# Channel mixers of a two-layer encoder trunk: chains T2 to T4 as products of 512 columns, their second half added by a transfer

## The chip, the core and the metric

The kernel runs on one core of a Trainium2 chip. The core has five engines with instruction streams of their own: TensorE (PE) multiplies 128x128 weight tiles with up to 512 columns and writes to the accumulator memory PSUM; VectorE (DVE) and ScalarE (ACT) do elementwise work, from and to the on-chip memory SBUF and PSUM; GpSimd (POOL) and SyncE (SP) mostly issue transfers (DMAs). Engines wait for each other through semaphores, and each runs its own instructions in order.

The metric is the device time of one execution in microseconds, the median of several runs. Lower is better.

## What is computed

Two transformer-like layers over 512 tokens of width 1024, batch 1, all in float32: a mixer (mLSTM or banded attention, each with attention to a memory), then a gated MLP with a causal convolution of width 3 over time. The change is in that MLP, the "channel mixer", which runs once per layer:

```python
def conv_ffn(h, w_up, conv_w, conv_b, w_down):
    u, g = jnp.split(h @ w_up, 2, axis=-1)      # w_up: 1024 x (2 * 2816)
    g = causal_dwconv(g, conv_w, conv_b)
    return (jax.nn.silu(g) * u) @ w_down        # w_down: 2816 x 1024

# in each layer:
x = x + conv_ffn(rmsnorm(x, norm_ffn_g[l]), ffn_w_up[l], ffn_conv_w[l], ffn_conv_b[l], ffn_w_down[l])
```

## The kernel before

**Three products for one.** TensorE's fast float32 form (fp32r) keeps fewer bits than float32, so each operand is split in a high part, a cast by ScalarE (`split`, L122), and a low part, the rest, a subtraction by VectorE (L123). `mm3` then issues three products: high by high (L166), high weights by low activations (L167) and low weights by high activations (L168).

**Tiles and steps.** Activations lie with the channels on the 128 partitions and the 512 tokens along the row. The 2816 hidden channels of a mixer are 22 tiles j. Tiles 0 to 4 are computed plainly (`plain`). From 5 on, `later` runs one `step` per tile, which computes the up and the gate block of the tile together by Winograd's variant of Strassen's scheme: the weights as 2x2 blocks (up and gate by two halves of the 1024 input channels), the activations as 2x2 blocks (two halves of the channels by two halves of 256 tokens), seven chains of products in place of eight. The weight forms are A11, A12, S1, S2, S3, A22 and S4 (class `Forms`); the sums of the activations are T1 to T4 (`forms`, with `self.sums`). One chain (`products`) is four `mm3` of 256 columns: twelve products.

**Accumulators of a step.** `r1` gathers A11 B11, then S2 T2, S3 T3 and A22 T4 on top of each other, and ScalarE copies its state to SBUF after each of the four (L796, L802, L812, L819). `r2` takes A12 B21; `r3` takes S1 T1 and later S4 B22. From the copies come `up` (the tile's up block) and `pre` (its gate block before the convolution). All three lie in banks of 512 columns, of which the chains use 256.

**The tail.** Step j finishes tile j-1 (class `Tail`): `last_block` adds `r3` to the second half of `up`; `first_tap` is ScalarE's scale and bias of `pre` (L652); `second_tap` and `third_tap` are VectorE's shifted multiply-adds (L645), the latter followed by the SiLU on ScalarE (L909); `gated` multiplies by `up` (L912); `split` splits the result for the down projection.

**Down projection.** In the steps that `DOWN` names (6 and 8 to 20) two blocks of twelve products of 512 columns run between the chains (`down_products`), one behind S2 T2 and one behind S3 T3. ScalarE copies each from PSUM (`add`, L735) and POOL issues a transfer that adds it to a spill in DRAM (L736). Steps 5, 7 and 21 have no such blocks. The last six hidden tiles are projected after the steps.

**Order.** Within the steps the order of PE, ACT and DVE is that of the code (`manual_schedule`): a step names the next tile's weight forms (`nxt`: `sums`, `split_second`, `sum_third`, `split_up`, `split_sums`, `sum_fourth`, `split_down`, `split_gate`, with subtractions at L847) and the tail's parts in their places. Where such an instruction would wait, the scheduler can put work that follows the steps in front of it. SP issues the weight loads; POOL issues the spills and, in the first mixer, at the start of each step the copies that lay out the bias rows of the attention (`bias_rows`, L1242 and L1244, of which the second waits for the first to land). Buffers come from pools: `t` has 8 tiles of 128x512, `bias` 4 (in the second mixer two of them hold the final gain), PSUM's `mm` 3, `sc` 3 and `tr` 2.

Of the kernel before, what the change touches and what calls it, by code (L numbers as in the profile page):

```python
# [16 lines left out]
P = 128  # L17
D = 1024
S = 512
# [32 lines left out]
def trunk(  # L52
# [572 lines left out]
    class ChannelMixer:  # L625
# [64 lines left out]
        def forms(self):  # L690
# [10 lines left out]
            for k in range(KT // 2):  # L701
                b1, b2 = xT[k], xT[k + KT // 2]
                pairs = []
                ta, tb = sb("t", [P, S]), sb("t", [P, S])
                for o, x, y in (
                    (ta[:, :H], b1[:, H:], b1[:, :H]),
                    (ta[:, H:], b2[:, H:], ta[:, :H]),
                    (tb[:, :H], b2[:, H:], b1[:, H:]),
                    (tb[:, H:], b2[:, :H], ta[:, H:]),
                ):  # L710
                    V.tensor_tensor(out=o, in0=x, in1=y, op=ALU.subtract)
                for t in (ta, tb):
                    hi, lo = sb("u", [P, S], F32R), sb("u", [P, S], F32R)
                    split(hi, lo, t)
                    pairs.append((hi, lo))
                self.sums.append(pairs)
                yield
# [41 lines left out]
        def t(self, i):  # L759

            i, h = divmod(i - 1, 2)
            return [tuple(x[:, h * H : (h + 1) * H] for x in p[i]) for p in self.sums]
# [22 lines left out]
        def step(self, j, w, nxt, tail):  # L785
# [5 lines left out]
            then(tail, "last_block", "first_tap")  # L791
            w.split_fourth()
            r1, r2, new.r3 = ps("mm"), ps("mm"), ps("sc")
            new.up, new.u3, new.pre = sb("t", [P, S]), sb("t", [P, S]), sb("t", [P, S])
            self.products(r1, w.a11, self.b(0, 0), True)
            A.copy(new.up[:, :H], r1[:, :H])  # L796
            then(tail, "second_tap")
            self.products(r2, w.a12, self.b(1, 0), True)
            V.tensor_tensor(out=new.up[:, :H], in0=new.up[:, :H], in1=r2[:, :H], op=ALU.add)
            then(tail, "third_tap")  # L800
            self.products(r1, w.s2, self.t(2))
            A.copy(new.up[:, H:], r1[:, :H])  # L802
            then(nxt, "sums")
            then(tail, "gated")
            then(nxt, "split_second", "sum_third")
            w.down_products(0)
# [4 lines left out]
            self.products(r1, w.s3, self.t(3))  # L811
            A.copy(new.u3[:, :H], r1[:, :H])  # L812
            V.tensor_tensor(out=new.pre[:, H:], in0=new.u3[:, :H], in1=new.r3[:, :H], op=ALU.add)
            then(nxt, "split_sums")
# [3 lines left out]
            self.products(r1, w.a22, self.t(4))  # L818
            A.copy(new.pre[:, :H], r1[:, :H])  # L819
            then(nxt, "split_down", "split_gate")  # L820
# [687 lines left out]
```

## Time and profile before

| | |
|---|---|
| median of three runs | 1209.37 us (1208.14 to 1210.49) |
| profiled execution | 1208.28 us, its span 1206.5 us |
| busy in the span | PE 99%, weight loads 87%, DVE 78%, ACT 59%, POOL 12% |
| granted TensorE clock, mean | 0.999 |
| transfers | 161.79 MB, 134 GB/s over the span |

The span runs from the first to the last instruction of the profiled execution; 1.8 us of its time lie around it. Rows of the timeline give the start in us, the duration, the engine, the line, the operation, the tiles out<-in, shapes, and in brackets the idle time ahead with what ended it. A product's duration reaches over the starts of the next ones, since products are pipelined; the distance from one start to the next is what a product adds to the time. Line numbers are those of the kernel before; `L166`, `L167`, `L168`, `L122`, `L123` are lines of helpers and stand for many places.

### The profile page before, as it was taken

To read this page: it belongs to the slowest core of one execution; us is meant where nothing else is said; L and a number is where in the kernel's file an instruction comes from. 1 tells how busy PE (TensorE), PEld (TensorE's weight loads), DVE (VectorE), ACT (ScalarE), POOL (GpSimd) and SP (SyncE) were. 2 spreads that over 40 slices of the span, in tenths; PEclk is the share of its full clock that TensorE was granted. 3 is DMA by queue.
4 is the path that set the end of the run, shared out by engine and by line. 5 is a ranking of instruction groups with operands and counts; after the bars stand their busy time and mean duration, and the time that the engine had idled before them with its cause. 6 is when DMAs were issued, how large, how long until landed. Compare 5 with 4: busy or idle time off the path is not lost.

```text
span 1206.5 us, 18758 instructions
## 1 busy us (share of the span) xinstructions
PE 1191.2 (99%) x7031; PEld 1055.1 (87%) x7031; DVE 938.8 (78%) x1719; ACT 711.9 (59%) x1253; POOL 139.5 (12%) x229
## 2 busy tenths in 40 slices
PE   8999999999999999999999999999999999999997
PEld 8898888888889999999888888888889999999986
DVE  6877688887978777777698888997896777777755
ACT  4547577654655555555565667775565555555545
POOL 0211101011011111111021000101101010111100
PEclk9999999999999999999999999999999999999999
DMA  8646413347565766665564313244845456666551
GB/s 277 200 112 144 91 54 79 109 147 193 123 151 141 161 159 147 153 145 130 148 193 129 93 53 101 68 132 153 194 101 135 114 131 140 141 140 135 121 156 70
DMA packets 206284, 161.79 MB, mean 134 GB/s; under 512 B 8328, under 2 KB 185966, under 8 KB 206194
## 3 DMA queue, kind: packets, MB, share of 16 engines
q1 hardware_dynamic: 184338, 120.78, 34.2%
q0 software_dynamic: 21856, 39.82, 17.7%
q8 instruction: 55, 0.90, 0.3%
q14 instruction: 35, 0.29, 0.1%
HBM read 132.04 MB, written 32.46 MB: 136 GB/s over the span
## 4 chain that ended last, share of the span: by engine, by line
PE 94%; ACT 3%; DVE 2%; DMA 0%; issue 0%; SPq 0%; DVEq 0%; ACTq 0%
PE pmm L166 18%; PE pmm L168 18%; PE pmm L167 18%; PE ptr L166 6%; PE ptr L167 6%; PE ptr L168 6%; PE psc L168 5%; PE psc L167 5%; PE psc L166 5%; PE psc L505 2%; PE ptr L1335 1%; ACT wh L122 1%; PE ptr L1356 1%; PE ptr L1357 1%; DMA u<-in_mem_dram 0%; PE ptr L574 0%
## 5 line engine op out<-in xcount | busy, mean ns | idle before, releaser
L166 PE MATMUL pmm<-u,wh 128*128 128x512 f32 (+1 forms) x968 | 336.6, 348 | 0.1
L168 PE MATMUL pmm<-u,wl 128*128 128x512 f32 (+1 forms) x968 | 333.5, 345 | 0.0
L167 PE MATMUL pmm<-u,wh 128*128 128x512 f32 (+1 forms) x968 | 333.2, 344 | 0.1
L123 DVE TENSOR_TENSOR wl<-wr,wh 128x1024 fp32r<-128x1024 f32 (+4 forms) x168 | 194.5, 1159 | 94.0 <-ACT wh L122 93.4
L122 ACT CAST wh<-wr 128x1024 fp32r<-128x1024 f32 (+4 forms) x168 | 167.7, 1000 | 96.1 <-PE pmm L167 42.1
L168 PEld LDWEIGHTS pmm<-u,wl 128*128 128x128 f32 x968 | 183.6, 190 | 21.1
L167 PEld LDWEIGHTS pmm<-u,wh 128*128 128x128 f32 x968 | 183.9, 190 | 18.4 <-DVE u L123 0.8
L166 PEld LDWEIGHTS pmm<-u,wh 128*128 128x128 f32 x968 | 183.7, 190 | 18.0 <-ACT u L122 0.5
L166 PE MATMUL ptr<-u,wh 128*128 128x512 f32 x272 | 106.7, 392 | 0.0
L167 PE MATMUL ptr<-u,wh 128*128 128x512 f32 x272 | 106.5, 392 | 0.0
L168 PE MATMUL ptr<-u,wl 128*128 128x512 f32 x272 | 105.8, 389 | 0.0
L736 POOL DMA_DIRECT2D xspill<-t x64 | 55.9, 873 | 411.6 <-ACT t L735 411.6
L166 PE MATMUL pmm<-u,u 128*128 128x256 f32 x296 | 84.5, 285 | 2.5 <-ACT t L812 2.5
L168 PE MATMUL pmm<-u,u 128*128 128x256 f32 x296 | 83.9, 284 | 0.2 <-DVE u L123 0.2
L167 PE MATMUL pmm<-u,u 128*128 128x256 f32 x296 | 83.8, 283 | 0.0
L123 DVE TENSOR_TENSOR u<-pt,u 128x512 fp32r<-128x512 f32 x102 | 69.9, 688 | 9.7 <-ACT u L122 7.1
L166 PE MATMUL psc<-u,wh 128*128 128x256 f32 (+1 forms) x232 | 76.1, 328 | 0.0
L735 ACT COPY t<-ptr 128x512 f32<-128x512 f32 x64 | 37.5, 585 | 65.4 <-PE ptr L168 65.4
L167 PE MATMUL psc<-u,wh 128*128 128x256 f32 (+1 forms) x232 | 75.9, 327 | 0.0
L123 DVE TENSOR_TENSOR u<-t,u 128x512 fp32r<-128x512 f32 x78 | 53.4, 689 | 22.0 <-ACT u L122 21.3
L122 ACT CAST u<-pt 128x512 fp32r<-128x512 f32 x102 | 63.0, 617 | 11.5 <-DVE pt L847 11.3
L909 ACT ACTIVATE t<-t 128x512 f32<-128x512 f32 x34 | 21.6, 634 | 80.3 <-DVE t L645 80.3
(282 smaller groups left out, 2562.5 us busy)
## 6 DMA issues: line engine op xcount, KB each, us to landing
wr<-in_ffn_w_up_dram SPq DMA_DIRECT2D x54, 512.0 KB, 4.9
wr<-in_ffn_w_down_dram SPq DMA_DIRECT2D x38, 512.0 KB, 3.8
pt<-in_ffn_w_up_dram SPq DMA_DIRECT2D x34, 512.0 KB, 6.7
xspill<-t POOLq DMA_DIRECT2D x64, 256.0 KB, 4.8
wr<-in_a_w_in_dram SPq DMA_DIRECT2D x20, 512.0 KB, 4.0
xspill<-u POOLq DMA_DIRECT2D x32, 256.0 KB, 2.9
u<-xspill SPq DMA_DIRECT2D x32, 256.0 KB, 5.2
wr<-in_w_kv_dram SPq DMA_DIRECT2D x12, 512.0 KB, 4.2
```

The lines of the kernel that those rows point to most:

```text
L122: high = A.copy(hi, src) if on_act else V.tensor_copy(hi, src)
L123: low = V.tensor_tensor(out=lo, in0=src, in1=f(hi), op=ALU.subtract)
L166: nc.tensor.matmul(o, lh, rh, start=first, stop=False, skip_group_check=more)
L167: nc.tensor.matmul(o, lh, rl, start=False, stop=False, skip_group_check=more)
L168: nc.tensor.matmul(o, ll, rh, start=False, stop=last, skip_group_check=more)
L505: nc.tensor.matmul(o, a, b, start=first and i == 0, stop=i == 1)
L735: A.copy(t, o)
L736: G.dma_start(xspill[j], t, accum_op=ALU.add)
L909: A.activation(self.acc, self.acc, AF.Silu)
L1335: nc.tensor.transpose(tp[:, b * P : (b + 1) * P], es[T, h][:, b * P : (b + 1) * P], ident)
L1356: nc.tensor.matmul(o2[:, s * P :], w, hi_at(pts[h], s, s, TT - s), start=s == 0, stop=False)
L1357: nc.tensor.matmul(o2[:, s * P :], w, lo_at(pts[h], s, s, TT - s), start=False, stop=s == TT - 1)
```

## The change

For tiles 5 to 20 of both mixers:

- The two parts of each of T1 to T4 now lie side by side in one tile of 512 columns (high in the first half, low in the second). For that, `forms` splits the sums in pieces of 256 columns.
- The chains of S2 T2, S3 T3 and A22 T4 are `wide_products`: per tile of input channels one product of the high weights with all 512 columns, and one of the low weights with the high half. The product of high weights and low activations gathers in the second half of `r1`'s bank.
- `fold` brings that second half in: ScalarE copies it to a `bias` tile (L774 of the changed kernel), and POOL issues a transfer that adds it to the destination in SBUF (L775): to the second half of `up` after T2, the second half of `pre` after T3, the first half of `pre` after T4.
- The parts of a step are reordered: the tail's `first_tap` and `second_tap` come behind the chain of T2, `third_tap` behind `split_second`; the next tile's `sums` come ahead of that chain, `sum_third` ahead of the first down block, `gated` behind it.

Tile 21 keeps the narrow chains, in the new order. PE has 6401 rows instead of 6785.

On ACT, step 7 of the first mixer (no down blocks), before. L796, L802 and L812 copy `r1` after A11 B11, S2 T2 and S3 T3; `t_3878` is the tail's tile, whose first tap stands ahead of this piece; `wh_3956` is the cast of `split_up`:

```order
L796 COPY t_3887<-pmm_3884 128x256
L909 ACTIVATE t_3878<-t_3878 128x512
L802 COPY t_3887<-pmm_3884 128x256
L122 CAST u_3935<-pt_3266 128x512
L122 CAST u_3952<-t_3878 128x512
L122 CAST wh_3956<-wr_3873 128x1024
L812 COPY t_3888<-pmm_3884 128x256
```

The same place in the changed kernel, where L821, L826 and L839 are those three copies, L774 the copies of `fold`, L652 the first tap and L938 the SiLU:

```order
L821 COPY t_3895<-pmm_3892 128x256
L826 COPY t_3895<-pmm_3892 128x256
L774 COPY bias_3935<-pmm_3892 128x256
L652 ACTIVATE t_3938<-t_3729,cols_772 128x512
L122 CAST u_3941<-pt_3266 128x512
L938 ACTIVATE t_3938<-t_3938 128x512
L122 CAST u_3961<-t_3938 128x512
L122 CAST wh_3965<-wr_3883 128x1024
L839 COPY t_3896<-pmm_3892 128x256
L774 COPY bias_3979<-pmm_3892 128x256
```

The first tap and the SiLU moved from ahead of the copy after T2 to behind it, and the copy after T3 has a second copy behind it.

On POOL, step 8 of the first mixer, before, from the second transfer of the step's bias rows on:

```order
L1244 DMA rep_4012<-maskf 64x64
L736 DMA xspill<-t_4108 128x512
L736 DMA xspill<-t_4151 128x512
L1242 DMA rep_4187<-in_b_rel_row_dram 128x640
L1244 DMA rep_4187<-maskf 64x64
```

The same place in the changed kernel, with the folds at L775:

```order
L1273 DMA rep_4019<-maskf 64x64
L775 DMA t_4035<-bias_4075 128x256
L736 DMA xspill<-t_4114 128x512
L775 DMA t_4037<-bias_4135 128x256
L736 DMA xspill<-t_4156 128x512
L775 DMA t_4037<-bias_4168 128x256
L1271 DMA rep_4191<-in_b_rel_row_dram 128x640
L1273 DMA rep_4191<-maskf 64x64
```

The three folds stand around the two spills, the first behind the bias rows' wait, the third ahead of the next step's bias rows.

Between the copies after T3 and T4 of step 21, PE had five products of the last down projection in the first mixer and six in the second; now it has nine and ten.

The diff:

```diff
@@ forms @@
-                for t in (ta, tb):
-                    hi, lo = sb("u", [P, S], F32R), sb("u", [P, S], F32R)
-                    split(hi, lo, t)
-                    pairs.append((hi, lo))
+                for t in (ta[:, :H], ta[:, H:], tb[:, :H], tb[:, H:]):
+                    both = sb("u", [P, S], F32R)
+                    split(both[:, :H], both[:, H:], t)
+                    pairs.append(both)
@@ t, wide_products, fold @@
         def t(self, i):
 
-            i, h = divmod(i - 1, 2)
-            return [tuple(x[:, h * H : (h + 1) * H] for x in p[i]) for p in self.sums]
+            return [(p[i - 1][:, :H], p[i - 1][:, H:]) for p in self.sums]
+
+        def wide_products(self, o, w, i):
+
+            n = KT // 2
+            for k in range(n):
+                both = self.sums[k][i - 1]
+                nc.tensor.matmul(o, w[0][:, k], both, start=False, stop=False, skip_group_check=True)
+                nc.tensor.matmul(o[:, :H], w[1][:, k], both[:, :H], start=False, stop=k == n - 1, skip_group_check=True)
+
+        def fold(self, to, o):
+
+            t = sb("bias", [P, S])[:, :H]
+            A.copy(t, o[:, H:])
+            G.dma_start(to, t, accum_op=ALU.add)
@@ step @@
             new = Tail(self, j)
-            then(tail, "last_block", "first_tap")
+            wide = j < FT - 1
+            then(tail, "last_block")
...
+            def chain(weights, i):
+                if wide:
+                    self.wide_products(r1, weights, i)
+                else:
+                    self.products(r1, weights, self.t(i))
+
+            def fold(to):
+                if wide:
+                    self.fold(to, r1)
+
             self.products(r1, w.a11, self.b(0, 0), True)
             A.copy(new.up[:, :H], r1[:, :H])
-            then(tail, "second_tap")
             self.products(r2, w.a12, self.b(1, 0), True)
             V.tensor_tensor(out=new.up[:, :H], in0=new.up[:, :H], in1=r2[:, :H], op=ALU.add)
+            then(nxt, "sums")
+            chain(w.s2, 2)
+            A.copy(new.up[:, H:], r1[:, :H])
+            fold(new.up[:, H:])
+            then(tail, "first_tap", "second_tap")
+            then(nxt, "split_second")
             then(tail, "third_tap")
-            self.products(r1, w.s2, self.t(2))
-            A.copy(new.up[:, H:], r1[:, :H])
-            then(nxt, "sums")
+            then(nxt, "sum_third")
+            w.down_products(0)
             then(tail, "gated")
-            then(nxt, "split_second", "sum_third")
-            w.down_products(0)
             self.products(new.r3, w.s1, self.t(1), True)
             w.add_down(0)
             then(tail, "split")
             then(nxt, "split_up")
-            self.products(r1, w.s3, self.t(3))
+            chain(w.s3, 3)
             A.copy(new.u3[:, :H], r1[:, :H])
             V.tensor_tensor(out=new.pre[:, H:], in0=new.u3[:, :H], in1=new.r3[:, :H], op=ALU.add)
+            fold(new.pre[:, H:])
             then(nxt, "split_sums")
             w.down_products(1)
             then(nxt, "sum_fourth")
             w.add_down(1)
-            self.products(r1, w.a22, self.t(4))
+            chain(w.a22, 4)
             A.copy(new.pre[:, :H], r1[:, :H])
+            fold(new.pre[:, :H])
             then(nxt, "split_down", "split_gate")
             self.products(new.r3, w.s4, self.b(1, 1))
```

## The prediction, made before the changed kernel was run

> **What bounds the kernel now.** I read the page first: busy times, granted clock and the chain that ended last.
>
> ```profile
> span 1206.5 us, 18758 instructions
> ...
> PE 1191.2 (99%) x7031; PEld 1055.1 (87%) x7031; DVE 938.8 (78%) x1719; ACT 711.9 (59%) x1253; POOL 139.5 (12%) x229
> ...
> PEclk9999999999999999999999999999999999999999
> ...
> PE 94%; ACT 3%; DVE 2%; DMA 0%; issue 0%; SPq 0%; DVEq 0%; ACTq 0%
> ```
>
> TensorE (PE) is busy for 99% of the span at full clock in all 40 slices, and 94% of the chain is its products. Busy time hides short waits, because one product's 0.28 us overlaps the next, so I then measured from one start to the next in the timeline of PE, over one step of the first channel mixer.
>
> ```profile
> 403.24 0.40 PE L166 MATMUL ptr<-u,wh 128*128 128x512 f32 x1
> ...
> 405.99 0.28 PE L166 MATMUL psc<-u,wh 128*128 128x256 f32 x1
> ...
> 407.42 0.28 PE L166 MATMUL pmm<-u,wh 128*128 128x256 f32 x1
> ...
> 418.80 0.40 PE L166 MATMUL ptr<-u,wh 128*128 128x512 f32 x1
> ```
>
> The rows at 403.24 and 405.99 enclose a block of the down projection: 12 products of 512 columns in 2.75 us, 0.229 us each. The rows at 405.99 and 407.42 enclose one chain: 12 products of 256 columns in 1.43 us, 0.120 us each. The row at 418.80 is the same place one step on, 15.56 us later. Seven chains and two down blocks are 7 x 1.44 + 2 x 2.75 = 15.58 us, so in such a step PE waits for nothing. The table by stage says the same of all the steps.
>
> ```profile
> 347.38:587.28 239.90, 238.65 (x1682) 224.40 (x1681) 183.65 (x268) 136.69 (x233) 38.77 (x53) 1.00 0.64 145
> 913.70:1153.60 239.90, 238.66 (x1682) 224.42 (x1681) 183.95 (x268) 136.90 (x234) 24.36 (x29) 1.00 0.57 130
> ```
>
> Each stretch runs from step 5 to the start of step 21 in one of the two mixers: 239.90 us each, PE busy 238.65. VectorE (DVE) is busy 183.65 and ScalarE (ACT) 136.69 of it. So PE's own time counts in full, ACT and DVE have room on average, and only a place where PE must wait for one chain of their work can cost anything.
>
> **What the merged products save.** Per chain of T2, T3 and T4, four products of 512 and four of 256 columns stand where twelve of 256 stood. The mean pitches give 4 x (0.229 + 0.120) = 1.40 against 1.44. A 512 right behind a 256 stands alone elsewhere in the trace.
>
> ```profile
> 221.32 0.28 PE L505 MATMUL psc<-u,u 128*128 128x256 f32 x1
> 221.43 0.40 PE L166 MATMUL pmm<-u,wh 128*128 128x512 f32 x1
> 221.67 0.52 PE L505 MATMUL psc<-u,u 128*128 128x256 f32 x3
> ```
>
> The 256 takes 0.11 and the 512 behind it 0.24 (the next row): 0.35 a pair, against 3 x 0.12 = 0.36. I take 0.35, so 0.04 us a chain and 0.12 us a step. The columns are the same, and only a fixed part of each product goes. The line through 0.120 at 256 and 0.229 at 512 puts that part at 0.011 us, which bounds the saving at 0.044 a chain; below, it is bounded by nothing saved. In the 28 steps with down blocks (14 in each mixer: 6 and 8 to 20) this is 28 x 0.12 = **-3.4 us** (ends -3.7 and 0).
>
> A rule speaks against even that. The Trainium skill, page "TensorE: Matmul & The Clock Gate", section "Wait — 56ns, not 53.3ns?", puts the fixed part of a product at about 2.5 ns at full clock. By it 384 fewer products would save an estimated 1.0 us, and the sum below would be about 2.5 us higher. The rows here speak for 0.011 us.
>
> **What the added copies and transfers cost in those steps.** Each step gains three ScalarE copies of 128x256, three transfers on GpSimd's (POOL) queue, and a later place for the tail's taps.
>
> ```profile
> 409.06 0.37 ACT L812 COPY t<-pmm 128x256 f32<-128x256 f32 x1 [0.82 <-PE pmm L168]
> 409.33 1.05 ACT L122 CAST wh<-pt 128x1024 fp32r<-128x1024 f32 x1
> ```
>
> The chain that began at 407.42 ended at 408.86, and the copy of its result starts 0.20 us behind it and gives way after 0.27. So 0.8 us of copies a step join ACT, which has over 6 us of room a step. Before a product overwrites a half, both copies must be done. In a step with down blocks the third chain is followed by 2.75 us of down products. Counted from the step's first product, T2's chain ends at 1.44 + 1.44 + 1.40 = 4.28 and the chain of T4 starts at 4.28 + 2.75 + 1.44 + 1.40 + 2.75 = 12.62 and the copies are done by 11.5 (worked out below for step 7, where they come at the same offset). They are hidden with 1.1 us to spare.
>
> The transfer behind T4's chain is the tight one, since the first tap of the next step waits for it.
>
> ```profile
> xspill<-t POOLq DMA_DIRECT2D x64, 256.0 KB, 4.8
> ...
> pt<-in_ffn_w_up_dram POOLq DMA_DIRECT2D x6, 512.0 KB, 7.2
> ...
> bias<-rep POOLq DMA_DIRECT2D x12, 256.0 KB, 3.2
> ```
>
> ```profile
> L736 POOL DMA_DIRECT2D xspill<-t x64: 850/859/944, 338.8 to 1150.9; - x64
> ...
> DMA to landing us min/median/max: 2.3/4.3/6.6
> ```
>
> None of these adds 128 KB from SBUF to SBUF. Adding 256 KB to DRAM lands after 4.8 us, adding 512 KB to SBUF after 7.2, a plain 256 KB into SBUF after 3.2. The line through the first two puts 128 KB at 3.6 us; the ends are 2.3 (fastest spill) and 7.2. I take 4.5, because the spill of add_down(1) is issued just ahead on the same queue. From T4's end to the issue it takes 0.20 + 0.27 + 0.37 = 0.84 us. The first tap could otherwise start 0.20 + 2 x 0.27 behind the chain of T2, which is 5.72 + 0.74 = 6.46 us after T4's end. So a landing up to 5.6 us after issue costs nothing, and with the 1.1 us above up to 6.7 us costs PE nothing. In the first mixer POOL also sits at a wait of its own.
>
> ```profile
> POOL rep L1244 <- DMA rep<-in_b_rel_row_dram: 62.6, 12, 6.3
> ```
>
> That is 12 waits, up to 6.3 us each, for the bias rows, now with the step's first fold queued behind them. The rows are issued behind the last fold, about 1 us into the step, so the first fold goes out near 8 us and lands near 12 of 15.4; its result is wanted at the next step's start. The cover is 3 us, so I cost it at nothing. The second fold waits for DVE's addition as well; behind it on POOL stands only the second spill, for which nothing waits in the step. Behind the first tap, should it wait, stand split_second's cast, the SiLU, a copy of the down block and so the whole tail.
>
> The finer splits of the sums (16 casts and 16 subtractions of 256 columns for 8 of each at 512, in each mixer) lie in the plain stage.
>
> ```profile
> 300.00:346.00 46.00, 46.00 (x206) 38.13 (x205) 40.52 (x67) 28.03 (x44) 4.78 (x5) 1.00 0.55 127
> ```
>
> PE is busy throughout it and DVE is idle for 5.5 of 46 us. On ACT a 256-column pass takes 0.27 to the next start where half of a 512 one takes 0.26 (rows above and below), and I estimate under 1 us in all on each engine. I cost that at nothing too; uncovered it would be 1 us.
>
> **Where the change loses.** Steps 5 and 7 of each mixer have no down blocks, so the chain of T4 follows that of T3 directly and waits for the copy of u3. Before, in step 7:
>
> ```profile
> 379.24 0.28 PE L168 MATMUL pmm<-u,wl 128*128 128x256 f32 x1
> 380.25 0.39 PE L166 MATMUL pmm<-u,u 128*128 128x256 f32 x1 [0.73 <-ACT t L812]
> ```
>
> The last product of T3's chain starts at 379.24 and ends its 0.12 at 379.36; T4's first starts at 380.25, 0.89 us of waiting for the copy at L812. Step 5 has the same place.
>
> ```profile
> 352.82 0.28 PE L168 MATMUL pmm<-u,wl 128*128 128x256 f32 x1
> 353.62 0.39 PE L166 MATMUL pmm<-u,u 128*128 128x256 f32 x1 [0.52 <-ACT t L812]
> ```
>
> Step 5 has no tail. There the fold's copy of 0.27 joins the wait of 0.68, and three chains save 0.12: **+0.15 us**, twice, +0.3.
>
> Step 7 has one, and the order of ACT has moved: the tail's first tap stands behind T2's copies instead of in front of the step, and the u3 copy still stands behind the SiLU, the tail's split and split_up. The durations come from step 7 of before.
>
> ```profile
> 376.76 0.63 ACT L909 ACTIVATE t<-t 128x512 f32<-128x512 f32 x1 [2.59 <-DVE t L645]
> ...
> 377.76 0.62 ACT L122 CAST u<-pt 128x512 fp32r<-128x512 f32 x1
> 378.36 0.62 ACT L122 CAST u<-t 128x512 fp32r<-128x512 f32 x1
> 378.88 1.04 ACT L122 CAST wh<-wr 128x1024 fp32r<-128x1024 f32 x1
> 379.83 0.36 ACT L812 COPY t<-pmm 128x256 f32<-128x256 f32 x1
> ...
> 383.71 0.81 ACT L652 ACTIVATE t<-t,cols 128x512 f32<-128x512 f32 x1
> 384.43 0.60 ACT L122 CAST u<-pt 128x512 fp32r<-128x512 f32 x1
> ```
>
> ```profile
> 375.65 0.74 DVE L645 SCALAR_TENSOR_TENSOR t<-t,cols,t 128x510 f32<-128x510 f32 x1
> 376.31 0.69 DVE L847 TENSOR_TENSOR pt<-pt 128x512 f32<-128x512 f32 x1
> ...
> 377.64 0.69 DVE L912 TENSOR_TENSOR t<-t,t 128x512 f32<-128x512 f32 x1
> ```
>
> On ACT: SiLU 0.63 (L909), cast to the next's start 0.52, the cast of 1024 columns 0.95 (378.88 to 379.83), first tap 0.81, L652. On DVE: a tap 0.74 or 0.66 to the next start (L645), a subtraction 0.60 to the next (376.31's kind), the gating product 0.69 (L912). From the step's first product: T2 ends at 4.28; its two copies run from 4.48 to 5.02; first tap to 5.83; second tap from 5.9 to 6.55; split_second's subtraction to 7.15; third tap to 7.9; SiLU to 8.55; gating to 9.3; tail's cast gives way at 9.85; split_up's at 10.8; u3's copy at 11.1; the fold's copy ends at 11.5. PE finished T3's chain at 4.28 + 1.44 + 1.40 = 7.12. It waits **4.4 us instead of 0.89**. Less the 0.12 saved, step 7 grows by 3.4 us. Adding pitches alone where I added full durations takes 0.6 off (2.8); hand-overs of 0.1 us instead of 0.05 put 0.3 on (3.7). PE has no idle later to give it back. Twice: **+6.8 us** (5.6 to 7.4).
>
> Step 21 keeps the narrow chains and its tail also comes later, but the scheduler fills that wait.
>
> ```profile
> 593.77 0.40 PE L167 MATMUL pmm<-u,wh 128*128 128x512 f32 x1
> 594.08 0.39 PE L166 MATMUL pmm<-u,u 128*128 128x256 f32 x1
> ```
>
> Five products of the last down projection stood there; the changed order has 9 in the first mixer and 10 in the second. They cover 9 x 0.229 = 2.06 us, up to 9.26 on the same clock, and the copy of u3 is done at about 9.4. I take +0.1 in all.
>
> **The sum.** -3.4 + 0.3 + 6.8 + 0.1 = **+3.8 us**. The profiled execution took 1208.28 us, a span of 1206.5 and 1.8 around it, so it would become 1212.1. That execution lies 1.1 below the median of the three runs, 1209.37; I predict the median, 1213.2. About 0.2% (2.4 us) is what a measurement of this kernel can tell from no change.
>
> **The rivals.**
> 1. The fixed part stays. If a 512 behind a 256 takes as long as two 256 (0.24, as in the row at 221.43, with 0.12 for the 256), nothing is saved in the 28 steps nor in steps 5 and 7: 3.8 + 32 x 0.12 = +7.6 us, 1217. Against it: the 256 ahead took 0.11 and the long runs 0.229. Chance 0.08. (The Trainium skill's 2.5 ns, page "TensorE: Matmul & The Clock Gate", would come out between this case and the forecast.)
> 2. The folds land late. If T4's transfer needs 7.2 us, as the 512 KB did, instead of under 6.7, the first tap, and with it the copies of u3, hold PE up 0.5 us in each of 28 steps: +14, 1227. For it: the spill landed after up to 6.6 us. Against it: half the bytes. Chance 0.13, most of it near the threshold (1214 to 1221).
> 3. On the other side: the weight load is what spaces the products of 256.
>
> ```profile
> L167 PEld LDWEIGHTS pmm<-u,wh 128*128 128x128 f32 x968 | 183.9, 190 | 18.4 <-DVE u L123 0.8
> ```
>
>    A load takes 0.19 us, longer than the pitch of 0.12, and a third of a chain's loads go. If a pair took 0.327, its columns at the slope of the line with no fixed part, a chain would save 0.132 and 96 chains 12.7 us: 7.6 - 12.7 = -5.1, 1204.3, faster. It decides from 0.08 us saved a chain (7.6 over 96). Against it: the lone pair at 0.35, and that 512-column products still carry the 0.011 although their loads have twice the time. Chance 0.05.
> 4. The wait in step 7 is mostly filled or shorter, so that gain and loss cancel: its added part would have to fall from 3.4 to below 2.7 us for less than 0.2%. The order of PE shows nothing between T3 and T4 there; only the times can do it. Together with the noise of a median, chance 0.14.
>
> **How the numbers follow.** My forecast has 0.60, with a range of its own of 1211 to 1215. With rivals 1 and the near part of 2 above it and part of 4 below, 1210.2 to 1218 leaves out about 0.2. Slower by over 0.2%: most of the forecast (0.55), rivals 1 and 2, 0.76. Within: 0.18, of rival 4 and the forecast's low end. Faster: rival 3 and a little of 4, 0.06.
>
> **What would show it.** Right: steps with down blocks of 15.43 to 15.45 us instead of 15.56; step 7 at about 14.6 us instead of 11.2, with T4's first product waiting over 4 us for ScalarE; a transfer of the fold landing in under 5.6 us with the first tap waiting for PE alone; 96 ScalarE copies without a wait of PE behind them elsewhere. Wrong: a down step above 15.6 us (folds late, or nothing saved at 15.56), or T4 in step 7 waiting under 3 us.

## The result, and the profile after

The changed kernel takes **1242.43 us** (median of five runs, 1236.80 to 1245.46) against 1209.37 before: a ratio of 1.0271 (95% interval 1.0255 to 1.0287), 33 us slower. The prediction had the sign, but said 1213.2 us, 1210.2 to 1218.0. The profiled execution of the changed kernel is the fastest of the five, 1236.80 us; its span of 1235.0 us is 28.5 us longer than the one before, and that is the part that the trace explains.

The page of the changed kernel, its lines on the span, the engines' busy time, the granted clock, the chain that ended last (by engine, then by line) and the folds' transfers (KB each, median us from issue to landing):

```profile
span 1235.0 us, 18341 instructions
...
PE 1199.1 (97%) x6647; PEld 1037.1 (84%) x6647; DVE 941.3 (76%) x1735; ACT 740.3 (60%) x1365; POOL 225.6 (18%) x325
...
PEclk9999999999999999999999999999999899999989
...
PE 60%; DMA 14%; issue 9%; DVE 8%; ACT 7%; POOL 2%; SPq 0%; ACTq 0%; POOLq 0%; DVEq 0%
...
t<-bias POOLq DMA_DIRECT2D x96, 128.0 KB, 3.5
```

PE's products were 94% of the chain and are 60%; transfers, which had 0%, hold 14%. PE is still 97% busy, and its busy time is even 8 us larger (1191.2 before): the clock fell in some slices, and a product at half clock counts as busy too. So the busy share hides most of this loss.

The table by stage, from step 5 to the start of step 21 in each mixer (length, then busy time of PE, PEld, DVE, ACT, POOL, granted clock, DMA share, GB/s):

```profile
346.82:596.39 249.57, 241.89 (x1490) 214.40 (x1489) 183.78 (x267) 149.08 (x280) 81.64 (x101) 0.99 0.77 162
926.16:1175.89 249.73, 241.15 (x1490) 214.45 (x1489) 183.79 (x266) 149.36 (x281) 66.34 (x77) 0.99 0.71 147
```

Each of these stages was 239.90 us. Going from one step's first ScalarE copy to the next one's, the extra 28.5 us lie as follows. "Down steps" are those with down blocks; "step 21" reaches to the next mixer's step 5, or to the end.

| us more than before | mixer 1 | mixer 2 |
|---|---|---|
| up to step 5 | -0.56 | (in step 21 of mixer 1) |
| step 5 (10.94 before) | +0.08 | +0.10 |
| step 7 (11.20 before) | +5.37 | +6.45 |
| down steps, 14 in each | +4.22 | +3.28 |
| step 21 and what follows | +3.35 | +6.20 |

**Down steps: the third fold lands late.** The place where one step passes to the next, mixer 2, in the timeline of POOL, then the landing time of the third of these transfers and of the spill ahead of it, then the next instruction on ScalarE that needs the third, then all such waits of ScalarE (total, times, longest):

```profile
1124.24 0.86 POOL L775 DMA_DIRECT2D t<-bias  x1 [2.83 <-ACT t L735]
1124.78 1.21 POOL L736 DMA_DIRECT2D xspill<-t  x1
1125.36 1.52 POOL L775 DMA_DIRECT2D t<-bias  x1
```

```profile
DMA to landing us min/median/max: 6.4/6.4/6.4
```

```profile
DMA to landing us min/median/max: 6.3/6.3/6.3
```

```profile
1131.79 0.82 ACT L652 ACTIVATE t<-t,cols 128x512 f32<-128x512 f32 x1 [1.01 <-DMA t<-bias]
```

```profile
ACT t L652 <- DMA t<-bias: 37.0, 26, 3.7
```

Second fold, spill and third fold are issued within 1.1 us. The third lands 6.4 us after its issue, at 1131.76, and the first tap (L652) starts at 1131.79. ScalarE waits there in 26 of 32 steps, 37 us in all. The spill, issued 0.58 us ahead of the fold, landed 0.7 us ahead of it. In 23 of the 28 steps with a spill it is the same: the third fold lands 0.6 to 1.0 us behind the spill issued ahead of it (1.2 to 2.1 in the others), whether that spill went out 0.6 or 1.5 us earlier. The spills themselves take 5.2 to 7.3 us. The length of a step follows from the landing of the third fold issued at the end of the step ahead of it. In mixer 2, with the landing first: 5.3 gives a step of 15.54 us, 6.4 gives 15.52 to 15.65 (five steps), 6.7 gives 15.87, 7.1 gives 16.30, 7.2 gives 16.35, 7.5 gives 16.64. (One lands after 6.1, but was issued 0.5 us later in its step: 15.77.) From about 6.4 us on, what the landing gains the step gains.

**Steps 7 and 21: PE waits, and then runs at half clock.** PE in the second mixer: the last product of T3's chain and the first of T4's in step 7, the last filling product and the first of T4's in step 21.

```profile
958.12 0.28 PE L769 MATMUL pmm<-u,wl 128*128 128x256 f32 x1
964.28 0.80 PE L768 MATMUL pmm<-u,u 128*128 128x512 f32 x1 [5.88 <-ACT bias L774]
...
1183.52 0.39 PE L166 MATMUL pmm<-wh,u 128*128 128x512 f32 x1
1187.71 0.58 PE L166 MATMUL pmm<-u,u 128*128 128x256 f32 x1 [3.81 <-ACT t L839]
```

The table by stage behind these two waits, and behind the shorter one of step 21 in the first mixer (2.98 us idle):

```profile
964.28:968.75 4.47, 4.46 (x20) 4.09 (x21) 2.76 (x4) 2.40 (x5) 1.42 (x2) 0.62 0.30 47
1187.71:1192.99 5.28, 5.28 (x24) 5.28 (x25) 2.10 (x4) 1.19 (x2) 0.00 (x0) 0.50 0.64 178
607.16:608.69 1.53, 1.53 (x12) 1.53 (x13) 0.94 (x3) 0.00 (x0) 0.00 (x0) 1.00 0.10 29
```

After 5.88 us of idleness the granted clock is 0.62 on average for 4.5 us (0.50 for the first 3.4), after 3.81 it is 0.50 for 5.3 us, after 2.98 it is 1.00. So the 6.2 us from step 21 of mixer 2 on are, to a few tenths, a wait of 3.8 and half of 5.3.

### The profile page after: what moved, and what is told of

It reads as the page before. It is cut to its first block, busy times and chain, and to the rows that moved or that the text cites. A ratio compares the mean times of both kernels' runs of the same rounds, so it can differ in the third digit from the quotient of the medians.

```text
span 1235.0 us, 18341 instructions
## 1 busy us (share of the span) xinstructions
PE 1199.1 (97%) x6647; PEld 1037.1 (84%) x6647; DVE 941.3 (76%) x1735; ACT 740.3 (60%) x1365; POOL 225.6 (18%) x325
## 4 chain that ended last, share of the span: by engine, by line
PE 60%; DMA 14%; issue 9%; DVE 8%; ACT 7%; POOL 2%; SPq 0%; ACTq 0%; POOLq 0%; DVEq 0%
DMA t<-bias 13%; PE pmm L166 11%; PE pmm L167 11%; PE pmm L168 11%; PE pmm L768 3%; PE psc L168 3%; PE psc L167 3%; PE psc L166 3%; PE ptr L166 3%; PE ptr L168 3%; PE ptr L167 3%; DVE t L645 3%; ACT wh L122 2%; PE psc L505 2%; ACT t L652 2%
## 5 line engine op out<-in xcount | busy, mean ns | idle before, releaser
L166 PE MATMUL pmm<-u,wh 128*128 128x512 f32 (+1 forms) x840 | 300.5, 358 | 0.1
L168 PE MATMUL pmm<-u,wl 128*128 128x512 f32 (+1 forms) x840 | 297.4, 354 | 0.0
L167 PE MATMUL pmm<-u,wh 128*128 128x512 f32 (+1 forms) x840 | 297.1, 354 | 0.1
L167 PEld LDWEIGHTS pmm<-u,wh 128*128 128x128 f32 x840 | 159.2, 190 | 18.2 <-DVE u L123 0.8
L166 PEld LDWEIGHTS pmm<-u,wh 128*128 128x128 f32 x840 | 159.1, 189 | 18.1 <-ACT u L122 0.5
L775 POOL DMA_DIRECT2D t<-bias x96 | 97.0, 1011 | 190.5 <-ACT bias L774 90.6
L645 DVE SCALAR_TENSOR_TENSOR t<-t,cols,t 128x511 f32<-128x511 f32 x80 | 59.7, 747 | 75.8 <-ACT t L652 75.7
L768 PE MATMUL pmm<-u,u 128*128 128x512 f32 x256 | 97.3, 413 | 16.3 <-ACT bias L774 15.8
L768 PEld LDWEIGHTS pmm<-u,u 128*128 128x128 f32 x256 | 49.1, 192 | 34.1 <-ACT bias L774 24.7
L769 PE MATMUL pmm<-u,u 128*128 128x256 f32 x256 | 72.9, 285 | 0.0
L123 DVE TENSOR_TENSOR u<-t,u 128x512 fp32r<-128x512 f32 (+1 forms) x94 | 53.9, 597 | 24.8 <-ACT u L122 24.4
L122 ACT CAST u<-t 128x512 fp32r<-128x512 f32 (+1 forms) x94 | 49.1, 544 | 23.6 <-DVE t L941 11.0
```

The costliest lines, as they stand in the source:

```text
L122: high = A.copy(hi, src) if on_act else V.tensor_copy(hi, src)
L123: low = V.tensor_tensor(out=lo, in0=src, in1=f(hi), op=ALU.subtract)
L166: nc.tensor.matmul(o, lh, rh, start=first, stop=False, skip_group_check=more)
L167: nc.tensor.matmul(o, lh, rl, start=False, stop=False, skip_group_check=more)
L168: nc.tensor.matmul(o, ll, rh, start=False, stop=last, skip_group_check=more)
L645: V.scalar_tensor_tensor(acc[:, n:], src[:, : S - n], self.fw[:, c * FT + j : c * FT + j + 1], acc[:, n:], op0=ALU.mult, op1=ALU.add,)
```

## The experiments

Three theories had to be told apart: the transfers of the folds, the new order of the step, and the merged products themselves. Times are medians; the ratio is against runs of the kernel before on the same chip (1208.75 us in the first four, 1208.21 in the next four, 1209.35 in the last two).

| run | us | ratio (95%) |
|---|---|---|
| 1 order only | 1219.29 | 1.0084 (1.0069 to 1.0099) |
| 2 no transfer | 1221.40 | 1.0100 (1.0085 to 1.0116) |
| 3 folds by VectorE | 1232.70 | 1.0195 (1.0178 to 1.0212) |
| 4 old steps 5 to 7 and 21 | 1215.52 | 1.0054 (1.0036 to 1.0072) |
| 5 no transfer, filler | 1216.06 | 1.0064 (1.0050 to 1.0078) |
| 6 spill later, first try | 1256.00 | 1.0388 (1.0366 to 1.0409) |
| 7 third fold by VectorE | 1220.72 | 1.0102 (1.0088 to 1.0116) |
| 8 old steps, third fold by VectorE | 1207.76 | 0.9998 (0.9989 to 1.0008) |
| 9 spill behind the third fold | 1222.72 | 1.0117 (1.0101 to 1.0132) |
| 10 old steps, spill behind the third fold | 1207.71 | 0.9994 (0.9985 to 1.0003) |

### 1. Order only

All chains narrow, no folds, the changed kernel's order.

```diff
-            wide = j < FT - 1
+            wide = False
```

> The changed kernel in its new order, but with narrow chains for every tile, so without merged products, copies and transfers of the fold. Theory O (the new order costs in the steps without down blocks): step 7 keeps a wait of about 4 us ahead of T4's chain and step 21 one of 1 to 3 us, down steps are 15.56 us, in all +6 to +12 us against before (ratio 1.005 to 1.010). Theory F (late folds cost everything): within 2.4 us of before. If the longer down blocks of the changed kernel (2.78 us for 2.74) come from the merged products ahead of them, they are back at 2.74.

Measured: 1219.29 us, 10.5 more than before. Steps 7 take 16.41 and 15.48 us instead of 11.20; T4 waits 3.66 us for ScalarE's copy of u3 (L839) in both, with half clock behind it (the chain of S4 takes 2.56 and 2.09 instead of 1.44). The same wait costs 0.9 us more in one mixer than in the other, as the granted clock stood at 0.50 for 6.8 us in the first and for 3.4 us in the second. Every down step is at 15.55 to 15.57, and the down blocks are back at 2.75 us. Step 21 is filled (0.18 us idle), so the 1 to 3 us expected there did not come. So the order alone costs its price in step 7, and nowhere else.

### 2. No transfer

Merged chains and the copies, but the second half is not added, so `up` and `pre` miss the low part of the sums.

```diff
             A.copy(t, o[:, H:])
-            G.dma_start(to, t, accum_op=ALU.add)
```

> The changed kernel without the 96 transfers of the fold; the copies from PSUM stay, and the second half's part of the sums is left out of the output. Theory F (the third fold lands late, 6.4 us after issue, and holds the first tap): the first tap waits for no transfer, down steps are 15.54 us in place of 15.86 in the mean, about 9 us below the changed kernel from these steps alone and some 2 more from step 7 and 21, so +20 to +23 us against before. Theory O alone: the down steps and the time stay at +33.

Measured: 1221.40 us, a ratio of 1.0100 where the changed kernel has 1.0271: the transfers cost some 21 us. It is 12.7 us above before where 20 to 23 were expected. In the profiled executions step 21 accounts for much of that: its 9.5 us more than before become 1.0, where some 2 us were expected of steps 7 and 21 together. The first copies of steps 8 and 20 of mixer 2, in run 1 and then in run 2:

```profile
960.62 0.37 ACT L821 COPY t<-pmm 128x256 f32<-128x256 f32 x1 [1.13 <-PE pmm L168]
...
1147.34 0.37 ACT L821 COPY t<-pmm 128x256 f32<-128x256 f32 x1 [0.52 <-PE pmm L168]
```

```profile
964.68 0.37 ACT L820 COPY t<-pmm 128x256 f32<-128x256 f32 x1 [1.67 <-PE pmm L168]
...
1151.16 0.37 ACT L820 COPY t<-pmm 128x256 f32<-128x256 f32 x1 [0.25 <-PE pmm L168]
```

Twelve steps take 186.72 us with narrow chains and 186.48 with merged ones: 15.56 and 15.54 a step. **The merged products save 0.02 us a step**, 12 products fewer at 1.7 ns each, instead of the 0.12 forecast. The merged chains themselves are shorter (T2 and T3 1.41 instead of 1.44, T4 1.40 instead of 1.43), but the down block behind T2 and the one behind T3 each take 2.78 instead of 2.75.

Step 7 of the first mixer, T3's last and T4's first product, and the table by stage from there on:

```profile
380.25 0.28 PE L769 MATMUL pmm<-u,wl 128*128 128x256 f32 x1
384.76 0.79 PE L768 MATMUL pmm<-u,u 128*128 128x512 f32 x1 [4.23 <-ACT bias L774]
```

```profile
384.76:390.05 5.29, 5.29 (x21) 4.90 (x22) 3.45 (x5) 3.22 (x6) 0.00 (x0) 0.50 0.23 75
390.05:392.92 2.87, 2.87 (x26) 2.87 (x25) 2.06 (x4) 0.68 (x2) 0.00 (x0) 1.00 0.48 148
```

The wait beyond the pitch of 0.12 is 4.38 us: the 4.4 of the prediction, to the hundredth or two. But then PE runs 5.3 us at half clock (6.1 in the other mixer), and the step takes 16.82 us (17.16 in the other mixer), not 14.6.

### 3. All folds by VectorE

```diff
-            t = sb("bias", [P, S])[:, :H]
-            A.copy(t, o[:, H:])
-            G.dma_start(to, t, accum_op=ALU.add)
+            V.tensor_tensor(out=to, in0=to, in1=o[:, H:], op=ALU.add)
```

> The changed kernel with the fold done by one VectorE addition from PSUM in place of the copy and the transfer. Theory F: as without transfers, +18 to +23 us against before, if VectorE's 3 x 0.33 us a step more stay hidden. Rival: VectorE is the next to hold PE, and the down steps stay above 15.7 us.

Measured: 1232.70 us. All down steps take 15.83 us. PE in one of them, the end of the second down block and the first product of T4, and then VectorE's addition of T3's second half:

```profile
1014.14 0.39 PE L168 MATMUL ptr<-u,wl 128*128 128x512 f32 x1
1014.61 0.47 PE L768 MATMUL pmm<-u,u 128*128 128x512 f32 x1
1014.91 0.28 PE L769 MATMUL pmm<-u,u 128*128 128x256 f32 x1
```

```profile
1012.38 1.22 DVE L123 TENSOR_TENSOR wl<-wr,wh 128x1024 fp32r<-128x1024 f32 x1 [0.26 <-ACT wh L122]
...
1014.04 0.42 DVE L773 TENSOR_TENSOR t<-t,pmm 128x256 f32<-128x256 f32 x1
```

T4's first product starts 0.47 us behind the last of the block instead of 0.23, and the next one 0.30 behind it instead of 0.24. T3's addition on VectorE (1014.04, 0.42 us) stands behind a subtraction of 1024 columns and ends at 1014.46; T4 may not write the half before that. So the rival holds, that VectorE is the next to hold PE: giving all folds to VectorE trades a late landing for a late release of the accumulator: 28 times 0.29 us, and a T4 wait of 5.77 us in step 7.

### 4. The old order in steps 5 to 7 and 21

Those steps narrow and in the order of before; tiles 8 to 19 merged with transfers; step 20 narrow in the new order.

```diff
-            wide = j < FT - 1
-            then(tail, "last_block")
+            wide = 8 <= j < FT - 2
+            old = j < 8 or j == FT - 1
+            then(tail, "last_block", *(["first_tap"] if old else []))
...
+            if old:
+                then(tail, "third_tap")
+                chain(w.s2, 2)
+                A.copy(new.up[:, H:], r1[:, :H])
+                then(nxt, "sums")
+                then(tail, "gated")
+                then(nxt, "split_second", "sum_third")
+                w.down_products(0)
+            else:
...
```

> Merged products and folds only for tiles 8 to 19; steps 5 to 7 and 21 in the order of before, the others in the new order. Theory O: step 7 is back at 11.2 us, step 21 waits for nothing beyond before, and PE is at full clock throughout; left over is the lateness of the folds, 12 steps in each mixer of about +0.3 us: +6 to +9 us against before. Theory F: the time stays within 6 us of the changed kernel.

Measured: 1215.52 us (1211.82 to 1219.35, a wide spread for this program). Steps 5 and 7 are back at 10.93 and 11.20. In the profiled execution the second mixer's steps 8 to 19 are all at 15.54, the first one's between 15.52 and 17.14. In the second mixer the third folds land in 5.2 to 5.8 us up to step 18, and no step is held up; the second spill goes out 1.2 to 1.9 us ahead of them. In the first mixer they land in 6.3 to 7.3 us from step 9 on, with the spill 0.6 us ahead. So the same steps run in two ways. My reading of the trace: a late tap makes the tail late, the second fold, which waits for VectorE's addition, goes out later, the spill behind it moves up to the third fold, and that fold lands late again; once begun, it keeps itself up. How it begins is not shown: in step 9 of the first mixer, the first with a late fold, the tap was on time and the second fold went out 0.8 us later in the step than in the second mixer all the same. The reading would also explain why the changed kernel's own runs spread over 8.7 us, where those without transfers spread over 2.7.

### 5. Products in place of idleness

Run 2, and in step 7 eighteen products ahead of T4's chain, whose results are not used.

```diff
             w.add_down(1)
+            if j == 7:
+                for _ in range(18):
+                    nc.tensor.matmul(r2, w.s1[0][:, 0], self.ready[0][0], start=True, stop=True)
             chain(w.a22, 4)
```

> The kernel without the fold's transfers (the second halves are not added), in which step 7 took 16.82 and 17.16 us and T4's chain waited 4.38 us in both mixers; now 18 products of 512 columns, whose results nobody reads, stand between the chains of T3 and T4 of step 7, 18 x 0.229 = 4.1 us of the wait. Theory 'half clock': TensorE, idle for 4.4 us, goes on at half clock (chain of T4 at 2.8 instead of 1.41 us, the next chain at 2.56 instead of 1.44), which costs 2.2 to 2.6 us a step 7 on top of the wait. With the filler it stays at full clock: step 7 takes 14.4 to 14.7 us in both mixers, the chains behind it 1.41 and 1.44, and the whole 1216 to 1217 us instead of 1221.4. Rival 'late operands': the chains behind the wait are slow because their weights or sums arrive late; then the filler changes nothing, step 7 stays at 16.8 to 17.2 and the whole at 1220 to 1223.

Measured: 1216.06 us, a ratio of 1.0064 for 1.0100. Step 7 takes 14.50 us in both mixers, 2.3 and 2.7 less than in run 2; every other step stays. PE's rows at the same place, and the table by stage (the products at L847 are the filler; the view begins behind the first two of them):

```profile
379.81 3.79 PE L847 MATMUL pmm<-u,wh 128*128 128x512 f32 x16
383.74 0.50 PE L768 MATMUL pmm<-u,u 128*128 128x512 f32 x1
```

```profile
383.74:386.70 2.96, 2.96 (x21) 2.77 (x21) 2.76 (x4) 2.13 (x4) 0.00 (x0) 1.00 0.03 8
```

T4's chain starts as long after T3's as without the filler (383.74 - 379.23 = 4.51, as 384.76 - 380.25), yet the clock stays at 1.00, and the two chains behind (T4's and S4's) take 2.96 us instead of 5.29. The late-operand rival falls: the operands come at the same time, and only PE's idleness is gone. **Half clock after the wait is 2.3 and 2.7 us a step 7** in run 2. (The Trainium skill, page "TensorE: Matmul & The Clock Gate", section "What's actually happening", says that an idle window of some 3.4 us halves the clock and a busy one of that length restores it. The runs agree on the fall in the main: none after 2.98 us (step 21), a fall after 3.30 (run 6, step 21), 3.66, 3.81 and 4.23. But once, in run 6, it fell after 1.90 us. At half clock PE worked for 3.2 to 6.1 us before the return, as the granted clock stood at 0.50 for 3.4 or 6.8 us at a time and part of that could lie in the wait.)

### 6. The second spill later, first try

The call that issues the second spill written behind the third fold, its copy left in place.

```diff
-            w.add_down(1)
+            spill = w.add_down(1, True)
...
             fold(new.pre[:, :H])
+            if spill is not None:
+                spill()
```

> The changed kernel, with the second spill of a step issued on POOL behind the third fold instead of 0.6 us ahead of it. Theory 'spill on the queue': the third fold lands late (median 6.4 us) because the 256 KB of the spill are ahead of it; it now lands in 3 to 5 us, the first tap no longer waits for it, down steps take 15.54 us in both mixers, and the whole 1220 to 1224 us, step 7 and its half clock being all that is left. Rival 'weight loads': the 512 KB loads that SP issues within 2.5 us of the fold make it late; it still lands in 6 us or more, and the whole stays at 1236 to 1245. Where both count, the landing falls to 5 to 6 us and the time lies between.

Measured: 1256.00 us, and the edit did not move the spill: POOL's order is the scheduler's, and the spill, whose copy was done first, was issued first all the same. What it moved instead was the first mixer's bias rows. POOL there, and the landing of the last row's fold (L923 is the spill, L1278 the bias rows):

```profile
457.44 1.20 POOL L923 DMA_DIRECT2D xspill<-t  x1
457.99 1.22 POOL L1278 DMA_DIRECT2D rep<-in_b_rel_row_dram  x1
458.56 1.54 POOL L775 DMA_DIRECT2D t<-bias  x1
```

```profile
DMA to landing us min/median/max: 7.9/7.9/7.9
```

With 320 KB of bias rows ahead of it too, the third fold lands in 7.8 to 8.6 us in steps 8 to 15 (6.2 to 7.3 in the changed kernel), and nine steps in a row take 16.8 to 19.2 us. (In the longest, step 12, the clock also fell to 0.50 for 3.4 us, after a PE wait of only 1.90.) The second mixer, which has no bias rows, stays as in the changed kernel (250.46 us for the stage, 249.73 before the edit). An experiment by accident: what stands ahead on POOL's queue makes the fold later.

### 7. The third fold by VectorE

```diff
-            fold(new.pre[:, :H])
+            V.tensor_tensor(out=new.pre[:, :H], in0=new.pre[:, :H], in1=r1[:, H:], op=ALU.add)
```

(For the wide steps alone; the other two folds stay transfers.)

> The changed kernel, but the third fold (behind T4's chain) is an addition by VectorE from the accumulator, 0.42 us, in place of copy and transfer; the other two folds stay transfers. Theory 'third landing': only the third transfer is late for its reader; down steps take 15.54 to 15.56 us, nothing of ScalarE waits for a fold's transfer, step 21 is filled again, and the whole is at 1220 to 1223 us, as without any transfer. Rival 'all the folds' or 'VectorE's time': the traffic of the other two, or the 0.33 us that join VectorE in each step, hold up the steps too: down steps at 15.6 us or more and the whole at 1226 or more (with all three folds on VectorE down steps took 15.83 and the whole 1232.7).

Measured: 1220.72 us. Every down step is at 15.54, no instruction of ScalarE waits for a fold, and step 21 is filled. Steps 7 remain, 16.53 and 16.76. So only the third transfer is late for its reader; the first two cost nothing, and 0.33 us more on VectorE a step cost nothing at this place, where PE does not wait for the addition.

### 8. Old steps 5 to 7 and 21, third fold by VectorE

Runs 4 and 7 together.

> The kernel with the old order and the narrow chains in steps 5 to 7 and 21 (merged chains in tiles 8 to 20 alone), and the third fold by VectorE. Theory 'third landing': steps 5 to 7 as before (10.94, 15.48, 11.20), down steps 8 to 20 at 15.54 us in both mixers against 15.56, so 26 x 0.02 = 0.5 us less than before at most: 1208.0 to 1210 us, the same as before within 0.2%. Rival 'the folds cost more than the products save even on time': down steps of 15.58 us or more in either mixer, and the whole above 1211.

Measured: 1207.76 us, ratio 0.9998 (0.9989 to 1.0008). Down steps 8 to 19 take 15.54 us in both mixers, and the stage from step 5 to step 21 takes 239.65 and 239.64 us against 239.90 before. With all the costs gone the merged products are worth a quarter of a microsecond a mixer, which a median of eleven runs doesn't show.

### 9. The second spill behind the third fold

ScalarE's copy of the second down block moved behind the fold's, so that POOL can only issue the spill after the third fold.

```diff
-            w.add_down(1)
             chain(w.a22, 4)
             A.copy(new.pre[:, :H], r1[:, :H])
             fold(new.pre[:, :H])
+            w.add_down(1)
```

> The changed kernel, with ScalarE's copy of the second down block moved behind the third fold's copy, so that POOL issues the second spill behind the third fold. Theory 'spill on the queue': the third fold lands late because 256 KB of spill were issued 0.6 us ahead of it; without them it lands in 2.8 to 5.5 us (2.8 and 3.3 in step 7, which has no spill, 5.3 and 5.5 in step 5, which has none but a weight load 0.2 us behind), the first tap stops waiting for it, down steps take 15.54 us in both mixers, step 21 is filled again, and the whole is at 1220 to 1224 us. Rival 'weight loads': the 512 KB loads issued within 2.5 us make it late; it lands in 6 us or more as before this edit and the whole stays at 1236 to 1245.

Measured: 1222.72 us. POOL at the passage from one step to the next in the second mixer, the landing of the fold at 1117.07, the next first tap on ScalarE, and all of ScalarE's waits for folds:

```profile
1114.90 0.86 POOL L775 DMA_DIRECT2D t<-bias  x1 [2.82 <-ACT wh L122]
1117.07 0.86 POOL L775 DMA_DIRECT2D t<-bias  x1 [1.31 <-ACT bias L774]
1117.61 1.21 POOL L736 DMA_DIRECT2D xspill<-t  x1
```

```profile
DMA to landing us min/median/max: 3.9/3.9/3.9
```

```profile
1122.39 0.83 ACT L652 ACTIVATE t<-t,cols 128x512 f32<-128x512 f32 x1
```

```profile
ACT t L652 <- DMA t<-bias: 1.9, 3, 1.1
```

The fold lands in 3.4 to 5.2 us in steps 8 to 19 of both mixers, 0.2 to 1.9 us ahead of the tap. Of the weight loads one goes out 0.9 us ahead of it and two 2.4 and 3.0 behind; in the undisturbed steps of run 4, where the spill was ahead and the fold took 5.2 to 5.8, it was 0.4 to 1.1 ahead and about 1.9 and 2.5 behind. So with the loads nearly where they were, moving the spill took the median landing from 5.6 to 3.9 us. But a load close by counts too. In step 5, with no spill ahead and a load 0.2 us behind, the third fold takes 5.2 and 5.1 us here, where step 7, with no load within a microsecond, has 2.8 and 3.2. At the end of step 20 it takes 6.2 and 5.6 us, and there a load goes out 0.04 us ahead of it and 0.2 behind; step 21 keeps a wait of 1.4 us at most. In the late steps of the changed kernel, too, the lateness had brought a load to 0.1 to 0.2 us behind the fold in most cases. What such a load costs where a spill stands ahead was not tried by itself. Moving one spill brings the ratio from 1.0271 to 1.0117, some 19 us; the order in step 7 is most of what is left (16.01 and 16.22 us; in the first mixer the wait is the 4.23 of run 2, and the step shorter because half clock lasted 3.4 us).

### 10. Old steps, and the spill behind the third fold

Runs 4 and 9 together: all three folds are transfers.

> As the run before, and with the old order and narrow chains in steps 5 to 7 and 21; all three folds are transfers. Theory 'spill on the queue': steps 5 to 7 at 10.93, 15.47 and 11.20, down steps 8 to 20 at 15.54 in both mixers, the whole at 1207 to 1210 us, the same as before within 0.2% (26 x 0.02 us saved). Rival 'weight loads' or 'bias rows' (in the first mixer POOL also moves 320 KB of bias rows right behind): down steps of 15.7 to 17 us in the first mixer, as with the spill ahead, and the whole at 1212 to 1219.

Measured: 1207.71 us, ratio 0.9994 (0.9985 to 1.0003). The stages take 239.65 and 239.66 us. The first mixer is as good as the second, bias rows or not. No version measured is faster than the kernel before by more than the measurement's uncertainty, and run 2 says why: there was 0.02 us a step to be had.

## Why the prediction was wrong

**The step that failed** is the landing of the third fold: "I take 4.5, because the spill of add_down(1) is issued just ahead on the same queue". The transfer was costed as one of its own, with 0.9 us added to the line's 3.6 for the spill. The runs show in its place that it lands 0.6 to 1.0 us behind the spill, and so at the spill's time and not its own: in 5.2 to 5.8 us while the steps run to plan (run 4), and 6.1 to 8.1 once they don't; with the spill behind it, in 3.4 to 5.2 (run 9). The spills of the kernel before took 3.8 to 6.5 us; the 2.3 that the prediction read as the fastest one stands in a view of all transfers to `xspill`. The bound drawn there was nearly right (cost from 6.7 us on; measured from about 6.4), and the prediction's second rival, at 0.13, is what happened. It was mis-priced too: it priced the 28 down steps alone at +14, where the profiled execution lost 7.5 us in them and 9.5 at step 21, at which the prediction looked only for the order. Two things were missed: that the lateness seems to keep itself up (run 4, argued and not shown), and that step 21, which has no down block, has no slack for it.

**Saved by merging, -3.4 us:** this term was mis-sized too: 0.02 us a step, -0.6 in 28. The pair of 256 and 512 at 0.35 was real, but what the chains of T2 and T3 gain, 0.03 us each, the down blocks behind them give back. The first rival, that nothing is saved, was the better forecast. (By the 2.5 ns of the Trainium skill, page "TensorE: Matmul & The Clock Gate", section "Wait — 56ns, not 53.3ns?", 12 products are an estimated 0.03 us a step; the measured 0.02 lies there, not at 0.12.)

**Step 7, +3.4 us each:** the mechanism and the wait were right (4.4 forecast, 4.38 measured without the transfers; the copy of u3 started 10.85 us into the step, for the 10.8 worked out), and with PE kept busy the step took 14.50 for the 14.6 forecast. Half clock, 2.3 and 2.7 us in run 2, was not in the sum. The trace of before held no wait of this length behind the kernel's start, and the prediction took PE's pitch as fixed. With the transfers the wait is, by the same count, 4.94 and 6.04 us, and the step 5.4 and 6.5 us longer than before.

**Step 5, +0.15 each:** 0.08 and 0.10. **Step 21, +0.1:** right while the tap is on time (0.18 us idle in runs 1 and 2), wrong with a fold that lands 7.5 and 8.1 us after its issue, at step 20's end: then the tap, the copy of u3 and T4 are late by 3 to 4 us.

**POOL's wait for the bias rows, at nothing:** right as a wait: in run 10 the first mixer runs like the second. But what the bias rows put on the queue counts where they go out ahead of the fold (run 6). **The plain stage, at nothing:** step 5 begins at 346.82 instead of 347.38.

So the sign came from step 7, where it was well argued. Most of the loss (some 21 of 33 us, run 2) came from transfers that were costed at nothing, the third one with one microsecond to spare, by a line through two transfers of other kinds.

## What to carry to other kernels

Here a transfer put on POOL's queue behind a larger one landed just behind it: cost it with what is ahead of it and with the loads issued beside it, and where its reader follows within a few microseconds, move the large one behind it (one moved spill was worth some 19 us here). Where a change opens a wait of PE of more than some 3 us (here 3.30 was always enough, 2.98 was not, and 1.90 was once), add the time at half clock behind it, or fill the wait with products. Before products are merged to save their fixed part, time a whole step with and without: 12 products fewer were worth 0.02 us, not the 0.12 that the pitches promised.

## What the runs showed of the hardware that was not expected

- Around PE waits of 3.30 to 6.59 us (runs 1 to 3, 6, 7, 9 and the changed kernel) the granted clock fell to 0.50 each time; around one of 2.98 us it did not. In run 6 it fell once after 1.90 us (PE back at 473.08, the fall at 474.43), and not after five other waits of 1.8 to 1.9 us. It stood at 0.50 for 3.4 or 6.8 us at a time, and the fall could come after PE had resumed (run 6: PE back at 623.81, the fall at 624.61). So equal waits cost differently: after 3.66 us, step 7 of run 1 took 16.41 and 15.48 us.
- An accumulating transfer of 128 KB within SBUF lands in 2.8 and 3.3 us in step 7 (no spill near it), in 5.1 to 5.5 with no spill but a 512 KB load 0.2 us behind it (step 5), in 3.1 to 5.2 with the spill behind it (runs 9 and 10), in 6.1 to 8.1 with 256 KB issued 0.5 to 1.1 us ahead on its queue, and up to 8.6 with 320 KB more ahead of it. With a spill ahead it landed 0.6 to 1.0 us behind that spill in 23 of 28 steps.
- A down block of 12 products of 512 columns takes 2.78 us behind a chain of alternating 512 and 256 columns, 2.75 behind a chain of 256. Why was not tried.
